# A decoder layer on one core: the mixer's VectorE work moved into PSUM, the division of the softmax moved behind the product with the values

## The chip, the cores and the metric

The kernel runs on one core of a Trainium2 chip. The metric is device time in microseconds (us) of one execution. A core has five engines that work side by side, each through its own instructions strictly in order: TensorE (PE in the profile, with its weight loads as PEld), VectorE (DVE), ScalarE (ACT), GpSimd (POOL) and SyncE (SP), which here issues the DMAs. Matmul results land in PSUM, eight banks of 128 partitions x 512 floats; everything else lies in SBUF.

## The reference, cut to what matters

A layer over 512 tokens of width 1024: a SwiGLU feed-forward network (FFN), a mixer, a second FFN, each with an RMSNorm in front and a residual add. The change is in the mixer alone:

```
p = rmsnorm(x) @ W_in                         # qa, ka, va, qi, ki, wi, cq, ckv, kr
qa, ka, qi, ki = rope(...)                    # x1*c - x2*s, x1*s + x2*c
# group A (Dsa): 8 query heads share one key/value head; an indexer of 16 heads picks 128 keys
score[t,s] = sum_h wi[t,h] * relu(qi[t,h] . ki[s])      # causal; top 128 keys of each query stay
out_A = softmax(qa . ka / 8 on the kept keys) @ va
# group B (Mla): 8 heads, queries and keys from low-rank latents, a shared rotary key
out_B = softmax((qn . kn + rope(qp) . rope(kr)) / sqrt(96), causal) @ v
x = x + concat(out_A, out_B) @ W_out
```

All arithmetic is float32. There are 4 query blocks of 128, so block i has (i+1) key blocks.

## The kernel before, in words

A product of two float32 matrices is done as three fast matmuls (`mm3`, L136, L139, L140) on operands that are cut into a high part (ScalarE rounds, L94) and a low part (the difference, L95 on VectorE or GpSimd). Every weight tile goes through this `split`. The products of probabilities and values and all transposes stay plain float32.

The FFNs lie before 393 us and after 700 us of the span; the mixer is between. Its order is written out by hand in `ORDER`: `q0`..`q7` are the index query projections (two heads of 64 each, for the three blocks that need an index: 384 tokens), `s0`..`s7` their rope and their stacking into operands, `i0`..`i7` the index heads, `T` and `k` the keys, `e` the rotary key, `l0`..`l4` the latents, `K`, `V` keys and values of group B, `A0`..`A3` and `S0`..`S3` the queries of group A, `b` rounds of the top-k search in the background. After the bar `|` come the 16 attention units (units 0 to 7 are Mla heads, 8 to 15 Dsa units, a block i and a half of the heads): `g` builds operands, `s` scores and softmax, `z` the division by the sum, `a` transposes of the probabilities and the product with the values, `o` parts of the output product. The tile framework then decides the order on each engine within what these dependences allow.

What the steps below touch:

- rope (L613 to L629): VectorE multiplies by the cosine out of PSUM into a buffer `f` (L619). The crossed halves times the sine come either from VectorE (L621, L622) or, after a ScalarE copy to SBUF, from GpSimd (L626, L627); the add (L628) is on either.
- stack and doubled (L637, L663): high part on ScalarE, low part on VectorE or GpSimd (L642, L669), quarters moved by DMA or by VectorE copies (L671).
- index heads (L692): two matmuls (L700, L701), relu on ScalarE from PSUM to a buffer `r` (L703, four buffers), multiply by the head's weight and accumulate on VectorE (L704).
- top-k (L709): 16 rounds of MAX8 and MATCH_REPLACE8 (L712, L713) on three score tiles, then L716.
- softmax (L855): VectorE adds mask or index and takes the maximum (L865), ScalarE exponentiates with the sum beside it (L873).
- normalise (L877): reciprocal (L880), then each block's probabilities are multiplied, on VectorE (L885) or GpSimd (L883).
- apply: transposes (L950 of Mla, L986 of Dsa), a copy to SBUF (L899 VectorE, L901 ScalarE), then the product: the values (64 columns) are loaded as weights and the transposed probabilities move, up to 512 columns (L953) or 256 (L991). The result is already turned (value dimension on partitions).

`ON_VECTOR` is a set of names that says which of two engines does an item.

Of the kernel before, what the change touches and what calls it, by code (L numbers as in the profile page):

```python
# [14 lines left out]
P = 128  # L15
# [10 lines left out]
BUFS = dict(pf=5, pr=4, ph=2, ah=7)  # L26
ORDER = """q0 q1 T c s0 r s1 t k q2 v w q3 i0 q4 a s2 i1 s4 q6 i2 q7 s3 q5 s6 s7 e s5 i3 l0 i4 i7 l1 i5 i6 l2 l3 l4 p b3 n0 u A0
A1 b2 K S0 A2 R b2 b2 S1 b2 A3 b3 S3 V S2 |
g0 s0 n1 g1 b2 g2 b2 s1 z0 s2 z1 b2 g3 g4 a0 s3 a1 b2 g5 z2 s4 a2 b2 z4 g6 z3 s5 g7 a3 s6 g8 z5 b2 b2 g9 a4 s7 g10 a5
b2 z6 s8 b2 a6 b2 b2 z7 a7 s9 o0 z8 g11 b2 b2 g12 b20 z9 b2 s10 z10 a8 s11 a9 a10 z11 g13 s12 o1 a11 g14 s13 z12 g15  # L30
s14 z13 s15 a12 z14 b2 o2 a13 a14 z15 a15 o3 o4 o5 b2 b2 o6 b2 o7 b2"""
ON_VECTOR = set("""c0.0 c0.1 c0.2 c0.3 c1.0 c1.2 c10.0 c11.0 c13.0 c14.3 c15.0 c15.1 c15.3 c2.1 c2.3 c3.1 c3.2 c3.3 c4.0 c4.3
c5.1 c6.0 c6.1 c6.2 c6.3 c7.2 gk5 gk7 kf mrA2 mrT mre mrq1 mrq2 mrq3 mrq5 mrq7 oa00 oa01 oa02 oa10 oa20 oa23
oa31 oa32 oa33 ob1 ob2 re rq1 rq2 rq3 rq5 ru1 sA2 sq6 sq7 su1 wA3 wV wl0 wl3 wo0 wo1 wo4 wo5 wo6 wo7 wq1 wq2
wq5 wq6 wq7 z0.0 z0.2 z0.3 z10.0 z10.2 z11.2 z12.0 z12.2 z12.3 z13.0 z13.2 z14.2 z14.3 z15.0 z15.1 z15.2 z2.3
z3.0 z3.1 z3.2 z3.3 z4.2 z4.3 z5.1 z5.2 z6.0 z6.2 z7.0 z7.1 z7.2 z7.3 z8.0 z9.0 z9.1""".split())
# [148 lines left out]
def rows_of(k, col, out):  # L185
    nc = k.nc
    pb = k.tr()
    for t in range(NT):
        nc.tensor.matmul(pb[:, t * P:(t + 1) * P], col[:, t:t + 1].to_broadcast([P, P]), k.ident, start=True, stop=True)
    nc.scalar.activation(out, pb, AF.Copy)  # L190
    return out
# [196 lines left out]
def engine(nc, name):  # L388

    return nc.vector if name in ON_VECTOR else nc.gpsimd  # L390


def add_mixer_weights(k, w_in, w_uq, w_ukv, w_out):
# [9 lines left out]
    lo = lambda name: engine(nc, "w" + name)  # L403
# [11 lines left out]
    def prep_keys():  # L415
        h, l = (w3(x, ND) for x in k.whl())
        for half in range(2):
            src = cell["t"][:, :, 0:128].rearrange("p d (h s c) -> p d h s c", h=2, s=2)[:, :, :, half, :]
            hv, lv = (x[:, :, 64 * half:64 * half + 64].rearrange("p d (h c) -> p d h c", h=2) for x in (h, l))
            k.split(hv, lv, src, lo("T"))  # L420
        return h, l

    def prep_rest():
        h, l = (w3(x, ND) for x in k.whl())
        for a, b, n in ((0, 208, 16), (16, 128, 16), (32, 144, 32), (64, 224, 16), (80, 128, 16), (96, 176, 32)):
            k.split(h[:, :, a:a + n], l[:, :, a:a + n], cell["t"][:, :, b:b + n], lo("t"))
# [4 lines left out]
    def rope_chunk(col, *names):  # L431
# [7 lines left out]
        def prep(j):  # L439
            def f():  # L440
                h, l = (w3(x, ND) for x in k.whl())
                for half in range(2):
                    src = c["r"][:, :, 128 * j:128 * j + 128].rearrange("p d (h s c) -> p d h s c", h=2, s=2)[:, :, :, half, :]
                    hv, lv = (x[:, :, 64 * half:64 * half + 64].rearrange("p d (h c) -> p d h c", h=2) for x in (h, l))
                    k.split(hv, lv, src, lo(names[j]))
# [11 lines left out]
    def plain(col, *names):  # L457
# [8 lines left out]
        def prep(j):  # L466
            def f():
                h, l = (w3(x, ND) for x in k.whl())
                k.split(h, l, c["r"][:, :, j * P:(j + 1) * P], lo(names[j]))
# [749 lines left out]
```

## Time and profile before

| | |
|---|---|
| runs, three | 1062.78 to 1064.68 us, median 1063.2 us |
| the profiled execution | 1066.48 us, of which its span is 1064.7 us |
| PE busy over the span | 1017.1 us (96%) |
| VectorE, ScalarE, GpSimd busy | 511.8, 385.2, 148.2 us |
| mixer | about 393 to 700 us of the span |

The profiled execution is one of its own; its span is what the trace covers, and 1.8 us lie around it. In the FFNs TensorE has no gaps; the stretches with gaps are those of the mixer. A busy share is not a bound: which wait ends last in a stretch is read from the chain of work that ended last.

### The profile page before, as it was taken

Reading aid. Unit: us, or ns where it says so; the run is one execution under the profiler, and the core shown is the slowest. Engines: PE = TensorE matmul, PEld = TensorE weight load, DVE = VectorE, ACT = ScalarE, POOL = GpSimd, SP = SyncE. Lnnn points to the kernel's source line nnn. Section 1 sums busy time; section 2 is a strip of 40 time slices with the busy share of each in tenths; the row PEclk is TensorE's granted clock in tenths of the full one; section 3 lists DMA queues with packets and bytes.
Section 4 is the critical chain, followed back from the end, with each engine's and each line's share of the span. In section 5 each row is a group of like instructions: output and inputs, shape, how many; then the busy total and the mean of one; then the engine's idle time right before and its main releaser. Section 6 shows DMA issues by size and latency. Waiting matters only on the chain.

```text
span 1064.7 us, 12212 instructions
## 1 busy us (share of the span) xinstructions
PE 1017.1 (96%) x4726; PEld 832.1 (78%) x4726; DVE 511.8 (48%) x895; ACT 385.2 (36%) x691; POOL 148.2 (14%) x142
## 2 busy tenths in 40 slices
PE   5999999999999999889889999999999999999997
PEld 3888888888888888768765566888888888888886
DVE  5333332333333336989996768553333233333343
ACT  5322221122222335654367556353222212222222
POOL 1000000000000026533984222000000000000000
PEclk9999999999999999989988999999999999999999
DMA  8232233223323123322251001243323232222302
GB/s 289 77 109 79 79 119 119 79 79 100 108 90 97 40 79 98 119 76 100 85 162 54 6 1 60 83 154 119 119 79 118 81 103 95 79 80 99 118 1 80
DMA packets 83391, 98.84 MB, mean 93 GB/s; under 512 B 9027, under 2 KB 65475, under 8 KB 83333
## 3 DMA queue, kind: packets, MB, share of 16 engines
q1 hardware_dynamic: 83328, 98.06, 28.7%
q8 instruction: 37, 0.61, 0.2%
q14 instruction: 22, 0.17, 0.1%
q10 hardware_dynamic: 4, 0.00, 0.0%
HBM read 91.89 MB, written 2.10 MB: 88 GB/s over the span
## 4 chain that ended last, share of the span: by engine, by line
PE 80%; DVE 12%; ACT 3%; issue 3%; DMA 1%; POOL 1%; SPq 0%; POOLq 0%; DVEq 0%; ACTq 0%
PE ps L136 24%; PE ps L139 24%; PE ps L140 24%; DVE idx L713 2%; DVE s L712 2%; DVE idx L704 1%; PE ps L953 1%; DVE wl L95 1%; DMA raw<-in_w_up_dram 1%; PE ps L991 1%; DVE p L885 1%; PE ps L986 1%; PE ps L950 1%; DVE p L865 1%; PE ps L975 1%
## 5 line engine op out<-in xcount | busy, mean ns | idle before, releaser
L94 ACT ACTIVATE wh<-raw 128x1024 fp32r<-128x1024 f32 (+4 forms) x154 | 140.1, 925 | 386.5 <-PE ps L139 297.4
L95 DVE TENSOR_TENSOR wl<-raw,wh 128x1024 fp32r<-128x1024 f32 (+1 forms) x122 | 145.0, 1192 | 277.3 <-ACT wh L94 276.9
L136 PE MATMUL ps<-xh,wh 128*128 128x512 f32 (+2 forms) x712 | 267.0, 379 | 5.1 <-DVE res L1123 1.7
L139 PE MATMUL ps<-xh,wh 128*128 128x512 f32 (+2 forms) x712 | 268.0, 377 | 1.9 <-DVE xh L95 1.9
L140 PE MATMUL ps<-xh,wl 128*128 128x512 f32 (+2 forms) x712 | 267.9, 377 | 1.3 <-POOL wl L95 0.9
L136 PEld LDWEIGHTS ps<-xh,wh 128*128 128x128 f32 x712 | 134.4, 190 | 30.0 <-DVE f L622 2.1
L140 PEld LDWEIGHTS ps<-xh,wl 128*128 128x128 f32 x712 | 135.1, 190 | 25.2 <-POOL wl L95 1.3
L139 PEld LDWEIGHTS ps<-xh,wh 128*128 128x128 f32 x712 | 135.2, 190 | 25.0 <-DVE xh L95 2.2
L136 PE MATMUL ps<-wh,h 128*128 128x512 f32 x272 | 105.9, 389 | 0.0
L140 PE MATMUL ps<-wh,h 128*128 128x512 f32 x272 | 105.8, 389 | 0.0
L139 PE MATMUL ps<-wl,h 128*128 128x512 f32 x272 | 105.8, 389 | 0.0
L95 POOL TENSOR_TENSOR wl<-raw,wh 128x512 fp32r<-128x512 f32 (+5 forms) x32 | 43.3, 1374 | 403.7 <-ACT wh L94 399.1
L327 DVE TENSOR_TENSOR t<-ps,t 128x512 f32<-128x512 f32 x44 | 30.4, 692 | 141.3 <-PE ps L140 141.3
L94 ACT ACTIVATE w<-raw 128x1024 fp32r<-128x1024 f32 x32 | 34.0, 1061 | 118.3 <-PE ps L139 118.3
L136 PE MATMUL ps<-xh,w 128*128 128x512 f32 x176 | 68.5, 389 | 0.0
L140 PE MATMUL ps<-xh,w 128*128 128x512 f32 x176 | 68.5, 389 | 0.0
L139 PE MATMUL ps<-xh,w 128*128 128x512 f32 x176 | 68.5, 389 | 0.0
L283 POOL TENSOR_TENSOR fr<-tot,mhalf 128x1 f32<-128x1 f32 x12 | 7.3, 614 | 415.6 <-DVE tot L1166 360.1
L140 PEld LDWEIGHTS ps<-wh,h 128*128 128x128 f32 x272 | 51.0, 188 | 10.7
L136 PEld LDWEIGHTS ps<-wh,h 128*128 128x128 f32 x272 | 51.1, 188 | 10.6
L139 PEld LDWEIGHTS ps<-wl,h 128*128 128x128 f32 x272 | 51.1, 188 | 10.5
L95 DVE TENSOR_TENSOR w<-raw,w 128x1024 fp32r<-128x1024 f32 x32 | 39.2, 1225 | 29.6 <-ACT w L94 29.6
(214 smaller groups left out, 1349.5 us busy)
## 6 DMA issues: line engine op xcount, KB each, us to landing
raw<-in_w_up_dram SPq DMA_DIRECT2D x22, 1024.0 KB, 5.2
raw<-in_w_gate_dram SPq DMA_DIRECT2D x21, 1024.0 KB, 5.2
raw<-in_w_down_dram SPq DMA_DIRECT2D x20, 1024.0 KB, 5.0
raw<-in_w_in_dram SPq DMA_DIRECT2D x8, 1024.0 KB, 5.2
raw<-in_w_out_dram SPq DMA_DIRECT2D x4, 1024.0 KB, 5.3
res<-in_x_dram SPq DMA_DIRECT2D x4, 512.0 KB, 7.0
raw<-in_w_down_dram SPq DMA_DIRECT2D x4, 512.0 KB, 3.6
raw<-in_w_ukv_dram SPq DMA_DIRECT2D x2, 1024.0 KB, 4.9
```

The costliest lines, as they stand in the source:

```text
L94: self.nc.scalar.activation(hi, src, AF.Copy)
L95: (lo_engine or self.nc.vector).tensor_tensor(out=lo, in0=src, in1=hi.bitcast(F32), op=ALU.subtract)
L136: i = mm(out, wh, xh, start=first, stop=False)
L139: mm(out, wh, xl, start=False, stop=False)
L140: return i, mm(out, wl, xh, start=False, stop=last)
L327: nc.vector.tensor_tensor(out=u, in0=pu, in1=g, op=ALU.mult)
L704: nc.vector.scalar_tensor_tensor(out=score[i], in0=r, scalar=wt[:, i, h:h + 1], in1=cm(i) if h == 0 else score[i], op0=ALU.mult, op1=ALU.add)
L712: nc.vector.max(out=m8, in_=score[i])
L713: nc.vector.match_replace(out=score[i], in_to_replace=m8, in_values=score[i], imm_value=TAKEN)
L865: nc.vector.tensor_tensor_reduce(out=e, in0=p[:, :n], in1=bias, scale=1.0, scalar=-3.0e38, op0=ALU.add, op1=ALU.max, accum_out=mx[:, c:c + 1])
L885: nc.vector.tensor_scalar(out=e, in0=e, scalar1=rc[:, c:c + 1], scalar2=None, op0=ALU.mult)
L950: nc.tensor.transpose(p[:, i * P:(i + 1) * P], probs[i][:, j * P:(j + 1) * P], k.ident)
```

## The change

1. Rope is done in place in PSUM, with four VectorE instructions: two halves times sine into `f`, the PSUM tile times cosine, the add. No rope has a ScalarE copy or a GpSimd part any more, except the rotary key `e`, which is wholly on GpSimd from an SBUF copy.
2. The index heads' relu is written back to PSUM and VectorE accumulates from there; the `r` buffers go.
3. The low parts of all mixer weights (L95 of `wl`) are on GpSimd; 15 of them were on VectorE.
4. The low parts of stacked and doubled operands, of `pe` and of group B's queries are on VectorE out of PSUM; group B's key low parts are all on GpSimd. Group B's queries stay in PSUM with no copy. The quarters of the keys' low parts are moved by ScalarE and by DMA.
5. The `z` step goes. The product runs on probabilities that are not divided; `divided` takes the reciprocal and multiplies the product's result on VectorE, 12 times (4 pairs of Mla heads, 512 wide, and 8 Dsa units, 256 wide).
6. In the product the transposed probabilities are the weights (128 x 128) and the values move (64 columns). The result has queries on partitions and is transposed afterwards: 16 transposes for Mla (new L944) and 16 for Dsa (new L985).
7. The attention's SBUF buffers `h` go from 7 to 8.

```diff
-    def rope(p, tab, name, n0=0):
+    def rope(p, tab, n0=0, eng=nc.vector):
...
-        nc.vector.tensor_tensor(out=a, in0=p, in1=c, op=ALU.mult)
-        if "m" + name in ON_VECTOR:
-            nc.vector.tensor_tensor(out=b[lower], in0=p[upper], in1=s[upper], op=ALU.mult)
-            nc.vector.tensor_tensor(out=b[upper], in0=p[lower], in1=s[lower], op=ALU.mult)
-        else:
-            x = f32()[:, n0:]
-            nc.scalar.activation(x, p, AF.Copy)
-            nc.gpsimd.tensor_tensor(out=b[lower], in0=x[upper], in1=s[upper], op=ALU.mult)
-            nc.gpsimd.tensor_tensor(out=b[upper], in0=x[lower], in1=s[lower], op=ALU.mult)
-        engine(nc, name).tensor_tensor(out=a, in0=a, in1=b, op=ALU.add)
-        return a
+        eng.tensor_tensor(out=b[lower], in0=p[upper], in1=s[upper], op=ALU.mult)
+        eng.tensor_tensor(out=b[upper], in0=p[lower], in1=s[lower], op=ALU.mult)
+        eng.tensor_tensor(out=p, in0=p, in1=c, op=ALU.mult)
+        eng.tensor_tensor(out=p, in0=p, in1=b, op=ALU.add)
+        return p
...
-                r = fr()[:, :n]
-                nc.scalar.activation(r, p, AF.Relu)
-                nc.vector.scalar_tensor_tensor(out=score[i], in0=r, scalar=wt[:, i, h:h + 1],
+                nc.scalar.activation(p, p, AF.Relu)
+                nc.vector.scalar_tensor_tensor(out=score[i], in0=p, scalar=wt[:, i, h:h + 1],
...
-            k.split(kh[r], kl[r], kf[pr][r], engine(nc, f"gk{h}"))
-            k.split(qh[r], ql[r], Mla.qf[r], engine(nc, f"gq{h}"))
+            k.split(kh[r], kl[r], kf[pr][r], nc.gpsimd)
+            k.split(qh[r], ql[r], Mla.qf[r])
...
-            po = Mla.po[64:128] if odd else Mla.po[0:64]
+            po = Mla.po.rearrange("p (i e c) -> p i e c", i=NT, e=2)
...
-                nc.tensor.matmul(po[:, j * P:], vb[j][:, h, :], t[:, j * P:], start=(j == 0), stop=(j == NT - 1))
+                for i in range(j, NT):
+                    nc.tensor.matmul(po[:, i, odd, :], t[:, i * P:(i + 1) * P], vb[j][:, h, :],
+                                     start=(odd == i == j == 0), stop=(odd == 1 and i == j == NT - 1))
             if odd:
+                o = divided(Mla.po, self.sm.rearrange("p a b -> p (a b)"))
+                p = k.tr()
+                for i in range(NT):
+                    nc.tensor.transpose(p[:, i * P:(i + 1) * P], o[:, i * P:(i + 1) * P], k.ident)
...
-                t = t.rearrange("p (a b q) -> p a b q", a=2, b=2)
-                for b in range(2):
-                    nc.tensor.matmul(po[64 * b:64 * b + 64, 0:256].rearrange("p (a q) -> p a q", a=2), va[:, j, :],
-                                     t[:, :, b, :], start=(j == 0), stop=(j == i))
+                for h in range(4):
+                    nc.tensor.matmul(po[:, 64 * h:64 * h + 64], t[:, h * P:(h + 1) * P], va[:, j, :], start=(h == j == 0), stop=(h == 3 and j == i))
+            o = divided(po, self.sm)
+            p = k.tr()
+            for e in range(2):
+                nc.tensor.transpose(p[:, e * P:(e + 1) * P], o[:, e * P:(e + 1) * P], k.ident)
+
+    def divided(po, sm):
+        rc = sums_of_two()
+        n = po.shape[1] // 64
+        rc = rc.rearrange("p a b -> p (a b)")[:, :n]
         nc.vector.reciprocal(out=rc, in_=sm)
...
+        o = turned()[:, :64 * n]
+        nc.vector.tensor_tensor(out=o.rearrange("p (a c) -> p a c", c=64), in0=po.rearrange("p (a c) -> p a c", c=64),
+                                in1=rc.unsqueeze(2).to_broadcast([P, n, 64]), op=ALU.mult)
+        return o
```

VectorE's order in the middle of the index heads before (`idx` are the score tiles, `r` the relu buffers, `ps` PSUM tiles, `wl` a weight's low part):

```order
L704 SCALAR_TENSOR_TENSOR idx_2657<-r_2909,wt,idx_2657 128x256
L704 SCALAR_TENSOR_TENSOR idx_2658<-r_2915,wt,idx_2658 128x384
L95 TENSOR_TENSOR wl_3032<-raw_2489,wh_3031 128x8x64 x2
L704 SCALAR_TENSOR_TENSOR idx_2659<-r_2921,wt,idx_2659 128x512
L704 SCALAR_TENSOR_TENSOR idx_2657<-r_2980,wt,idx_2657 128x256
L619 TENSOR_TENSOR f_3129<-ps_2863,tab_2644 128x384
L704 SCALAR_TENSOR_TENSOR idx_2658<-r_2986,wt,idx_2658 128x384
L704 SCALAR_TENSOR_TENSOR idx_2659<-r_2992,wt,idx_2659 128x512
```

And the same place after, where two ropes run among the accumulations:

```order
L612 TENSOR_TENSOR f_2994<-ps_2924,tab_2644 64x384
L613 TENSOR_TENSOR f_2994<-ps_2924,tab_2644 64x384
L612 TENSOR_TENSOR f_3101<-ps_2863,tab_2644 64x384
L613 TENSOR_TENSOR f_3101<-ps_2863,tab_2644 64x384
L614 TENSOR_TENSOR ps_2924<-ps_2924,tab_2643 128x384
L686 SCALAR_TENSOR_TENSOR idx_2656<-ps_2964,wt,idx_2656 128x256
L686 SCALAR_TENSOR_TENSOR idx_2657<-ps_2969,wt,idx_2657 128x384
L614 TENSOR_TENSOR ps_2863<-ps_2863,tab_2643 128x384
L686 SCALAR_TENSOR_TENSOR idx_2658<-ps_2974,wt,idx_2658 128x512
L615 TENSOR_TENSOR ps_2924<-ps_2924,f_2994 128x384
```

The weights' low parts have left VectorE, the ropes' other halves and adds have come, and the accumulations read PSUM tiles.

TensorE's order in two Dsa units before (`p` are probabilities, `h` the copied transposes, `va` the values, `kah` and `kal` the keys of the next scores):

```order
L986 MATMUL ps_4947<-ident,p_4820 128x128 x4
L991 MATMUL ps_4946<-h_4952,va 64x256 x2
L986 MATMUL ps_4961<-ident,p_4891 128x128 x4
L991 MATMUL ps_4960<-h_4966,va 64x256 x2
L986 MATMUL ps_4970<-ident,p_4891 128x128 x4
L975 MATMUL ps_4989<-kah,qa_3861 128x384
L976 MATMUL ps_4989<-kal,qa_3861 128x384
```

And after, a Dsa unit of two key blocks, from its first transpose to the next unit's scores:

```order
L977 MATMUL ps_4989<-ident,p_4868 128x128 x4
L981 MATMUL ps_4988<-va,h_4994 128x64 x4
L977 MATMUL ps_5000<-ident,p_4868 128x128 x4
L981 MATMUL ps_4988<-va,h_5005 128x64 x4
L985 MATMUL ps_5015<-ident,h_5013 128x128 x2
L965 MATMUL ps_5022<-kah,qa_4032 128x384
L966 MATMUL ps_5022<-kal,qa_4032 128x384
```

The product takes four instructions in the order (each is two passes on the engine) where it took two, and the unit ends with transposes (L985) of what VectorE divides; nothing stands between the last product and them.

## Rows read from the trace of the kernel before

**Rows 1.** Windows: us, busy (x) of PE, PEld, DVE, ACT, POOL; PEclk, DMA, GB/s.

```profile
426.00:480.00 54.00, 45.94 (x218) 39.01 (x217) 49.59 (x66) 31.75 (x66) 23.95 (x15) 0.94 0.35 101
480.00:557.00 77.00, 68.85 (x321) 56.71 (x320) 76.94 (x190) 36.78 (x61) 57.61 (x46) 0.96 0.37 115
557.00:602.00 45.00, 41.64 (x193) 26.82 (x192) 35.53 (x115) 31.34 (x84) 19.83 (x22) 0.91 0.13 37
602.00:680.00 78.00, 73.25 (x394) 51.65 (x395) 48.30 (x140) 38.94 (x113) 13.61 (x17) 1.00 0.15 48
```

**Rows 2.** Chain that ended last, by line, in those four windows.

```profile
by line: DVE idx L704 23.6%; issue 22.5%; DVE wl L95 6.6%; PE ps L700 5.0%; PE ps L701 4.4%; ACT r L703 4.2%; PE ps L139 4.1%; PE ps L136 4.1%; PE ps L140 3.8%; DVE f L619 3.7%; DMA qst<-h 3.4%; DVE f L622 3.1%; DVE h L642 2.5%; DVE f L628 
by line: DVE idx L713 29.4%; DVE s L712 24.9%; DVE wl L95 9.3%; issue 8.2%; DVE idx L716 4.4%; DVE f L619 4.1%; DVE kf L792 3.0%; DVE idx L704 2.9%; DVE p L865 2.1%; DVE lat L735 1.8%; ACT wh L94 1.5%; DVE f L628 1.3%; DVE scol L611 1.3%; P
by line: DVE p L885 21.6%; PE ps L953 12.6%; PE ps L950 11.4%; ACT p L873 10.9%; DVE p L865 10.4%; PE ps L935 6.6%; PE ps L936 5.2%; PE ps L937 5.1%; DVE h L899 3.8%; DMA st<-pe 3.8%; issue 3.6%; SPq L632 2.5%; DVE s L880 1.0%; ACT h L901 0
by line: PE ps L136 14.0%; PE ps L139 13.7%; PE ps L140 13.5%; PE ps L991 12.7%; PE ps L986 11.0%; PE ps L953 10.0%; PE ps L975 7.2%; PE ps L976 6.0%; ACT h L901 3.5%; PE ps L950 3.0%; DVE h L899 2.5%; ACT p L94 1.3%; DVE res L1123 0.9%; is
```

**Rows 3.** VectorE where the attention begins.

```profile
554.43 1.48 DVE L716 TENSOR_SCALAR idx<-idx 128x512 f32<-128x512 f32 x1
555.83 0.28 DVE L865 CUSTOM_DVE_ANT_0 p<-ps,cmask 128x128 f32<-128x128 f32 x1
```

**Rows 4.** VectorE before the first accumulation: start, us, what.

```profile
420.57 0.68 DVE L95 TENSOR_TENSOR wl<-raw,wh 128x512 fp32r<-128x512 f32 x1
...
422.33 1.58 DVE L671 CAST kil<-kil 32x512 fp32r<-32x512 f32 x2
...
424.20 0.85 DVE L671 CAST kal<-kal 32x512 fp32r<-32x512 f32 x2
425.08 1.30 DVE L95 TENSOR_TENSOR wl<-raw,wh 128x512 fp32r<-128x512 f32 x2
426.29 1.67 DVE L704 SCALAR_TENSOR_TENSOR idx<-r,wt,cmask 128x256 f32<-128x256 f32 x3
```

**Rows 5.** VectorE by form, 426.25 to 556.9: instruction xcount | busy us, mean ns | idle before.

```profile
L704 DVE SCALAR_TENSOR_TENSOR idx<-r,wt,idx 128x512 f32<-128x512 f32 x15 | 14.8, 988 | 0.0
L704 DVE SCALAR_TENSOR_TENSOR idx<-r,wt,idx 128x384 f32<-128x384 f32 x15 | 12.0, 800 | 0.1
...
L704 DVE SCALAR_TENSOR_TENSOR idx<-r,wt,idx 128x256 f32<-128x256 f32 x15 | 10.0, 670 | 0.0
...
L95 DVE TENSOR_TENSOR wl<-raw,wh 128x1024 fp32r<-128x1024 f32 x5 | 8.3, 1669 | 0.8 <-ACT wh L94 0.8
...
L95 DVE TENSOR_TENSOR wl<-raw,wh 128x512 fp32r<-128x512 f32 x5 | 4.4, 904 | 0.0
L619 DVE TENSOR_TENSOR f<-ps,tab 128x512 f32<-128x512 f32 x6 | 4.0, 672 | 0.0
...
L619 DVE TENSOR_TENSOR f<-ps,tab 128x384 f32<-128x384 f32 x5 | 2.8, 551 | 0.0
L621 DVE TENSOR_TENSOR f<-f,tab 64x512 f32<-64x512 f32 x1 | 2.7, 2710 | 0.1
...
L735 DVE SCALAR_TENSOR_TENSOR lat<-ps,g_q_lat,lat 128x512 fp32r<-128x512 f32 x3 | 2.2, 742 | 3.3 <-ACT lat L734 3.3
...
L619 DVE TENSOR_TENSOR f<-f,tab 128x512 f32<-128x512 f32 x1 | 0.7, 693 | 0.0
```

**Rows 6.** TensorE: a product of Mla, weight loads of transposes, products of Dsa.

```profile
578.99 1.07 PE L953 MATMUL ps<-h,xh 128*64 128x512 f32 x2 [0.32 <-ACT h L901]
...
598.65 1.07 PEld L950 LDWEIGHTS ps<-ident,p 128*128 128x128 f32 x10 [0.17 <-issue]
...
624.53 0.65 PE L991 MATMUL ps<-h,va 128*64 128x256 f32 x4 [0.69 <-ACT h L901]
```

**Rows 7.** TensorE's waits, 600 to 680: us in total, times, longest.

```profile
PE ps L991 <- ACT h L901: 2.4, 3, 1.0
PE ps L991 <- DVE h L899: 1.7, 2, 0.9
```

More of the change, by code (lines that the diff above doesn't have):

```diff
@@ L182, in rstd_of, with rows_of @@
     return col, m
-def rows_of(k, col, out):
+def rows_of(k, col, out=None):
     nc = k.nc
@@ L189, in rows_of @@
         nc.tensor.matmul(pb[:, t * P:(t + 1) * P], col[:, t:t + 1].to_broadcast([P, P]), k.ident, start=True, stop=True)
+    if out is None:
+        return pb
     nc.scalar.activation(out, pb, AF.Copy)
@@ L401, in w3 @@
         return x.rearrange("p (a b) -> p a b", a=a)
-    lo = lambda name: engine(nc, "w" + name)
+    lo = nc.gpsimd
     cell = {}
@@ L635, in quarters, with stack @@
         return [x[32 * q:32 * q + 32] for q in range(4)]
-    def stack(x, make, name, n0=0):
+    def stack(x, make, n0=0):
         out = [make()[:, n0:] for _ in range(2)]
         l = f32r()[:, n0:]
-        nc.scalar.activation(out[0], x, AF.Copy)
-        engine(nc, name).tensor_tensor(out=l, in0=x, in1=out[0].bitcast(F32), op=ALU.subtract)
+        k.split(out[0], l, x)
         nc.scalar.activation(out[1], x, AF.Copy)
@@ L661, in mixer, with doubled @@
     cm = lambda i: k.cmask[:, 384 - P * i:]
[L663 removed]
+    def doubled(x, hi, lo, q, copy):
         o = 1 - q
[L666 removed]
+        k.split(hi, lo, x)
         for e in (0, 2):
             nc.scalar.activation(quarters(hi)[o + e], quarters(x)[q + e], AF.Copy)
[L669 removed]
         for e in (0, 2):
[L671 removed]
+            copy(quarters(lo)[o + e], quarters(lo)[q + e])
     def values(x):
@@ L685, in rotary_key @@
     def rotary_key(x):
-        scaled(tk, v.rows1)
-        x = rope(x, tk, "re")
+        x = rope(x, v.tk, 0, nc.gpsimd)
         h, l = f32r(), f32r()
@@ L755, in norm_rows @@
     def norm_rows(j):
-        v.rows1 = rows_of(k, v.col1, row_tile())
+        rows = rows_of(k, v.col1)
+        v.ta = scaled(ta, rows, True)
+        v.tk = scaled(tk, rows)
     def index_keys(j):
-        v.ta = scaled(ta, v.rows1, True)
-        v.x1 = rope(v.t1, v.ta, "rT")
-        doubled(v.x1, kih, kil, 1, nc.vector)
-    def attention_keys(j):
-        doubled(v.x1, kah, kal, 0, nc.gpsimd)
+        x = rope(v.t1, v.ta)
+        doubled(x, kih, kil, 1, lambda o, i: nc.scalar.activation(o, i, AF.Copy))
+        doubled(x, kah, kal, 0, mv)
     def rest_out(j):
@@ L774, in index_stack @@
     def index_stack(j):
-        stacks[j] = stack(rope(pq.pop(j), ta, f"rq{j}", P), qst, f"sq{j}", P)
+        stacks[j] = stack(rope(pq.pop(j), ta, P), qst, P)
     def keys_b(j):
@@ L790, in keys_b_out @@
             x = mp.tile([P, T], F32, tag="kf", name=k.name("kf"), bufs=8)
-            if "kf" in ON_VECTOR:
-                nc.vector.tensor_tensor(out=x, in0=p, in1=rows, op=ALU.mult)
-            else:
-                nc.scalar.activation(x, p, AF.Copy)
-                nc.gpsimd.tensor_tensor(out=x, in0=x, in1=rows, op=ALU.mult)
+            nc.vector.tensor_tensor(out=x, in0=p, in1=rows, op=ALU.mult)
             kf.append(x)
@@ L812, in rotary_b_out @@
         for g, p in enumerate(v.pab):
-            x = rope(p, tb, f"ru{g}")
+            x = rope(p, tb)
             h, l = (mp.tile([P, T], F32R, tag="kf", name=k.name("pe"), bufs=8) for _ in range(2))
-            k.split(h, l, x, engine(nc, f"su{g}"))
+            k.split(h, l, x)
             pe.append((h, l))
@@ L829, in stack_a @@
     def stack_a(j):
-        qa[2 * j], qa[2 * j + 1] = stack(rope(pa.pop(j), v.ta, f"rA{j}"), mkqa, f"sA{j}")
+        qa[2 * j], qa[2 * j + 1] = stack(rope(pa.pop(j), v.ta), mkqa)
     def values_b(j):
@@ L853, in mixer, with softmax @@
     turned = k.junk = lambda: ap.tile([P, T], F32, tag="h", name=k.name("h"), bufs=BUFS["ah"])
-    def softmax(scores, scale, neg=None):
-        mx, sm, nb = (small(4) for _ in range(3))
+    def softmax(scores, sm, scale, neg=None):
+        mx, nb = (small(4) for _ in range(2))
         out = []
@@ L938, in score @@
                 out.append((p, cm(i)))
-            self.probs = softmax(out, *v.scale_b)
+            if h % 2 == 0:
+                Mla.sm = sums_of_two()
+            self.sm = Mla.sm
+            self.probs = softmax(out, self.sm[:, :, h % 2], *v.scale_b)
         def apply(self):
@@ L1010, in out_part @@
             out_done(t, half, p, part == 0)
-    do = dict(g=lambda j: units[j].gather(), s=lambda j: units[j].score(), z=lambda j: normalise(j),
+    do = dict(g=lambda j: units[j].gather(), s=lambda j: units[j].score(),
               a=lambda j: units[j].apply(), o=out_part, n=lambda j: k.weights(ids[f"n{j}"]), b=background)
```

76 lines of the change are left out of this document (29 added, 47 removed).

## The prediction

> **What bounds the kernel now.** First I read which engine works in each stretch of the mixer, in windows [rows 1]. From 480 to 557 us VectorE is busy 76.94 of 77.00 us; from 426 to 480 it is busy 49.59 of 54, TensorE 45.94. From 602 on the picture turns: TensorE 73.25 of 78 us, VectorE 48.30. Between (557 to 602) TensorE has 41.64 of 45 us, VectorE 35.53. [...]
>
> Busy shares don't say who sets the end, so I then read the chain of waits of each window [rows 2]. From 426 to 480 its longest part is VectorE's accumulations L704 (23.6%) and the low parts L95 (6.6%); from 480 to 557 it is the top-k (L713 29.4%, L712 24.9%) and L95 (9.3%). From 557 to 602 the largest part is the normalise pass L885, 21.6% of 45.0 us = 9.7 us. From 602 on TensorE's own lines follow one another and no line of the division is named in what the row shows. So there are three stages: VectorE bounds to 557, VectorE and ScalarE between TensorE's work bound to 602, TensorE bounds from there. The change relieves the first two and loads the third.
>
> That the first stage hands on what it gains is seen where the attention begins [rows 3]: the last top-k instruction L716 starts at 554.43, and the first maximum L865 follows it at 555.83 on the same in-order engine. Whatever VectorE finishes earlier, the attention starts earlier.
>
> **The change part by part.** *Before the first accumulation.* In the 5.7 us ahead of 426.29 VectorE does 0.68 + 1.30 us of weights' low parts and 1.58 + 0.85 us of quarter copies [rows 4], 4.4 us that all leave it (GpSimd, ScalarE and DMA take them). ScalarE's quarter copies now stand before the first index matmul. I take -4 us; bounds 0 (something else is as late, GpSimd's weights first) and -5.
>
> *The VectorE stage, 426.25 to 556.9.* What leaves: 10 low parts of weights, 8.3 + 4.4 = 12.7 us [rows 5]. What comes: 61 instructions of rope, stack, `pe` and group B's query low parts where 30 stood; 31 more at 0.55 us (the 384-wide multiply out of PSUM, 551 ns; the 512-wide takes 672) are +17, and the one 64x512 multiply of 2710 ns, whose sources lie in SBUF, is then an ordinary 0.7: -2. Net +15. What gets cheaper: the 45 accumulations take 988, 800 and 670 ns with both sources in SBUF; an instruction of the same kind with one source in PSUM, L735 at 128x512, took 742 ns in the same stretch, in which GpSimd was busy most of the time (57.61 of 77 us, [rows 1]). So I price the 512-wide accumulation out of PSUM at 0.74, and the narrower ones by the step of the multiplies (672 - 551 = 121 ns) at 0.62 and 0.50: 15 x (0.25 + 0.18 + 0.17) = -9. Sum: -12.7 + 15 - 9 = -7. The rows overlap a little at their ends, so I count -6 of time. If the accumulations don't get cheaper it is about +2; if L716 (1.48 us for the widest, [rows 3]) loses its surplus over the multiply's 0.67 as well, in two or three instructions, it is -9.
>
> GpSimd gets 15 more weights' low parts and loses its share of the ropes, of the stacks and of the normalise blocks (30 of 64). It is busy 57.61 of 77 us at its worst, so I cost that at nothing; what hides it is that weights are prepared two items ahead. If that cover is gone, TensorE waits for low parts, and the 12.7 us that VectorE spent on ten of them bound it; with 19 us of GpSimd idle in that window I leave this end out of the range.
>
> *Attention of Mla, 557 to 602.* The normalise pass leaves the chain: -9.7 us at most. The product of probabilities and values: a pair of passes over 512 columns takes 1.07 us [rows 6], 2.1 ns a column, so 8 heads x 1280 columns are 21.4 us. After it there are 80 products of two passes that are limited by the weight load; ten loads of 128x128 take 1.07 us [rows 6], so 160 x 0.107 = 17 us, and with the entry into each group of them some 20: -1. The 16 new transposes are 16 x 0.107 = +1.7. Each pair of heads now ends with a reciprocal and a 512-wide multiply that TensorE waits for, since its next instructions are those transposes; waits for one copy were 0.7 to 1.0 us [rows 6, 7], so two instructions and two hand-offs are about 1.2, four times: +4.8. The sum is -4. Bounds: -9.7 (waits hidden) and +6 (L885 lay beside TensorE work that ends just behind it).
>
> *Attention of Dsa and output product, from 602.* The products of 256 columns took 0.65 us for a group of four [rows 6], and there are 20 groups: 13.0 us. After it, 160 passes x 0.107 = 17.1, and an entry of 0.04 for each group: +4.9. New transposes: 16 x 0.107 = +1.7. Then waits. Before, 5 of the 20 groups waited for their copy, 2.4 + 1.7 = 4.1 us in all [rows 7], 0.8 each (one of 0.69 stands in [rows 6]). After, the order puts each product straight behind its transposes and each unit's final transposes straight behind its last product, with the reciprocal and the multiply between, eight times. I take half of the eight to be exposed at 0.8: +3.2. The sum is +10. Bounds: +5 (the waits hidden and the loads a little better) and +20 (all eight and ten more copies exposed).
>
> *Sum.* -4 - 6 - 4 + 10 = -4 us. The profiled execution was 1066.48 us (span 1064.7 and 1.8 around it), which makes it 1062.5; the median of the runs lies 3.3 lower, and there the forecast is **1059 us**.
>
> [...]
>
> **The rivals.** (1) *The tail decides.* In the Dsa units every copy and every division is exposed, because TensorE is the bound there and nothing is queued between. Its place is from 602 on, its price +20 in place of +11, and it decides as soon as more than the -14 of the first stages is given back: -14 + 20 = +6, 1069 us. For it: the order, and chain rows that are TensorE's alone. Against it: only a quarter of the copies are exposed before, with the same pairs of instructions.
>
> (2) *The gain is not handed on.* PSUM tiles are held longer (through four rope steps and two copies of the stack, through the relu, and the queries through two heads), there are eight banks, and TensorE starves or VectorE waits for products late. Then the first two terms give -3 in place of -10: +3, 1066 us. For it: TensorE already loses time from 426 to 480, and the chain has 22.5% issue there. Against it: TensorE has 8 us free in each of these two windows.
>
> (3) *Everything is hidden.* The division runs beside other units, the Dsa stage costs +5, Mla gives -8, the first two terms -11: -14, and less of the attention runs at the lower clock: 1046 to 1049 us. For it: the largest part of the chain from 557 to 602 leaves VectorE. Against it: VectorE's in-order queue puts the division behind maxima of later units.
>
> [...]
>
> **How the numbers follow.** Forecast case 0.42 (1059, own range 1053 to 1065), rival 1 0.22, rival 2 0.14, rival 3 0.17, rival 4 0.05. Runs of this kernel differ by 0.2%, 2 us, so faster means under 1061.1 and slower over 1065.3. Of the forecast case 0.29 lie below, 0.09 within and 0.04 above; rival 3 is all faster; of rivals 1, 2 and 4 together 0.05 faster, 0.07 the same, 0.29 slower. That makes faster 0.51, the same 0.16, slower 0.33. The range runs from rival 3's middle, 1047, to a little over rival 1's, 1071.
>
> **What would show each step.** Accumulations out of PSUM at 0.48 to 0.75 us beside a busy GpSimd, and the first L865 near 546 us of the span, show the first stage right. Means of 0.8 to 1.0 us, or VectorE idle in 426 to 546, would show it wrong. The product's weight loads at 0.107 each, in groups of four to sixteen, show the loads; gaps before the new transposes, 12 in all, and before the products show the waits. The forecast is wrong if the first L865 does not move, if those gaps add up to over 15 us, or if the attention stretch grows by less than 3 us.

## The result and the profile after

The changed kernel takes 1094.5 us (median, 1093.6 to 1098.4) against 1063.7 for the kernel before on the same chip: ratio 1.0297, interval 1.027 to 1.0323. It is 31 us slower, and the forecast was 1059. Its profiled span is 1091.8 us, 27.1 longer than before.

First the place. These are VectorE's rows where the accumulations begin and where the attention begins (start, us, what), answering [rows 4] and [rows 3]:

```profile
417.34 1.01 DVE L686 SCALAR_TENSOR_TENSOR idx<-ps,wt,cmask 128x256 f32<-128x256 f32 x2 [0.76 <-ACT ps L685]
...
544.08 0.29 DVE L843 CUSTOM_DVE_ANT_0 p<-ps,cmask 128x128 f32<-128x128 f32 x1
```

The first accumulation comes at 417.3 in place of 426.3, the first maximum at 544.1 in place of 555.8, 11.7 us earlier. Not all of that is the change's. The same residual add near the end of the first FFN, which the change doesn't touch, stands here in the two traces (before, then after):

```profile
385.17 0.69 DVE L363 SCALAR_TENSOR_TENSOR res<-ps,res 128x512 f32<-128x512 f32 x1 [2.03 <-PE ps L140]
```

```profile
381.87 0.69 DVE L362 SCALAR_TENSOR_TENSOR res<-ps,res 128x512 f32<-128x512 f32 x1 [2.03 <-PE ps L137]
```

The profiled execution of the kernel before was 3.3 us late already there; two kernels that are the same up to that point (e6 and e7 below) have this add at 382.5 and 382.6. So the change gains 11.7 - 3.3 = 8.4 us by the time that the attention starts (forecast 10), and all the loss lies behind.

The next rows are windows of the stretch from the first maximum to the last transposes of the normed input of the second FFN, of the kernel before and of the changed one (us from:to, us, busy of PE, PEld, DVE, ACT, POOL, granted clock, DMA share, GB/s):

```profile
555.83:702.54 146.71, 136.10 (x710) 96.99 (x711) 101.85 (x293) 80.86 (x222) 36.84 (x43) 0.97 0.19 59
```

```profile
544.08:726.41 182.33, 155.47 (x890) 136.39 (x891) 84.28 (x260) 79.53 (x216) 22.04 (x15) 0.88 0.13 40
```

The stretch is 35.6 us longer. VectorE and GpSimd do less in it, as meant. TensorE is busy 19.4 us more and idle 16.2 us more (182.33 - 155.47 = 26.9 against 10.6). The windows of the changed kernel that lie wholly at one level show a granted clock of 1.00 (589.33 to 623.46) or of 0.50 (two are below); a mean of 0.88 between these two means that 2 x 0.12 x 182 = 44 us of it ran at the lower level; before it was 2 x 0.03 x 147 = 9 us. (After the stretch the two kernels do the same FFN; in the changed one 3.2 us of its first products fall behind the end of the stretch, so from the first maximum on the loss is 35.6 + 3.2 = 38.8 us; 38.8 - 8.4 = 30.4 agrees with the 31 of the runs.)

TensorE's waits in it (us in total, times, longest), answering [rows 7]:

```profile
PE ps L981 <- ACT h L881: 6.7, 7, 3.0
PE ps L985 <- DVE h L864: 4.1, 8, 0.5
PE ps L981 <- DVE h L879: 3.5, 4, 0.9
PE ps L938 <- ACT h L881: 3.4, 2, 2.6
PE ps L938 <- DVE h L879: 3.3, 3, 1.4
PE ps L944 <- DVE h L864: 3.1, 4, 0.8
```

L985 and L944 wait for the division (7.2 us, all twelve times), L981 and L938 for a copy of transposes (16.9 us). How that looks is seen in TensorE's timeline, in the first and the third of three Dsa units:

```profile
614.83 0.60 PE L977 MATMUL ps<-ident,p 128*128 128x128 f32 x4
616.12 1.10 PE L981 MATMUL ps<-va,h 128*128 128x64 f32 x8 [0.69 <-ACT h L881]
617.74 0.44 PE L985 MATMUL ps<-ident,h 128*128 128x128 f32 x2 [0.52 <-DVE h L864]
...
622.15 0.60 PE L977 MATMUL ps<-ident,p 128*128 128x128 f32 x4
623.53 1.97 PE L981 MATMUL ps<-va,h 128*128 128x64 f32 x8 [0.78 <-DVE h L879]
625.29 1.06 PE L977 MATMUL ps<-ident,p 128*128 128x128 f32 x4
627.04 1.97 PE L981 MATMUL ps<-va,h 128*128 128x64 f32 x8 [0.69 <-ACT h L881]
629.52 0.69 PE L985 MATMUL ps<-ident,h 128*128 128x128 f32 x2 [0.52 <-DVE h L864]
```

Transposes, a wait, the product, a wait, transposes of the result: in these units the engine stands still before each product and before the last transposes. In the kernel before, other products often stood in that place:

```profile
619.69 0.60 PE L986 MATMUL ps<-ident,p 128*128 128x128 f32 x4
620.04 0.48 PE L136 MATMUL ps<-wh,ob 128*128 128x512 f32 x1
...
621.06 0.63 PE L140 MATMUL ps<-wh,ob 128*128 128x512 f32 x2
621.61 0.65 PE L991 MATMUL ps<-h,va 128*64 128x256 f32 x4
```

That product, the first of the Dsa units, starts 65.8 us after the first maximum, and 72.0 us after it in the changed kernel (616.12 above). The matmuls ahead of it are the same but for the new form of the product and its transposes. So the Mla stage lost 6.3 us and everything behind it 32.6.

In the rows of the changed kernel, from 623 on the same eight passes take 1.97 us in place of 1.10, and four transposes 1.06 in place of 0.60: the clock has fallen to the lower level. Two windows of the changed kernel lie wholly there, each behind a long wait for a copy of transposes:

```profile
574.78 3.76 PE L938 MATMUL ps<-xh,h 128*128 128x64 f32 x20 [2.56 <-ACT h L881]
```

```profile
654.42 1.97 PE L981 MATMUL ps<-va,h 128*128 128x64 f32 x8 [3.00 <-ACT h L881]
```

```profile
575.67:589.33 13.66, 12.09 (x52) 11.11 (x52) 4.46 (x14) 4.02 (x11) 0.00 (x0) 0.50 0.01 2
...
654.18:667.83 13.65, 12.89 (x47) 11.31 (x48) 3.87 (x13) 4.75 (x13) 0.00 (x0) 0.50 0.00 1
```

So the clock fell behind waits of both kinds: behind the five of 0.5 to 0.8 us ahead of 623.5 in the Dsa units, and behind single waits for copies of 2.6 and 3.0 us.

The product itself grew too. Its rows in the stretch (instruction xcount | busy us, mean ns | waits), before and after:

```profile
L953 PE MATMUL ps<-h,xh 128*64 128x256 f32 (+3 forms) x64 | 21.6, 457 | 2.0 <-DVE h L899 1.7 <-ACT h L901 0.3
...
L991 PE MATMUL ps<-h,va 128*64 128x256 f32 x80 | 11.4, 396 | 4.1 <-ACT h L901 2.4 <-DVE h L899 1.7
```

```profile
L981 PE MATMUL ps<-va,h 128*128 128x64 f32 x160 | 25.1, 316 | 10.3 <-ACT h L881 6.7 <-DVE h L879 3.5
L938 PE MATMUL ps<-xh,h 128*128 128x64 f32 x160 | 22.2, 293 | 6.7 <-ACT h L881 3.4 <-DVE h L879 3.3
```

It keeps TensorE busy for 47.3 us in place of 33.0, part of it at the lower clock, and waits for copies for 16.9 us in place of 6.1.

### The profile page after: what moved, and what is told of

It is laid out like the page before. It is cut to its first block, busy times and chain, and to the rows that moved or that the text cites. A ratio compares the mean times of both kernels' runs of the same rounds, so it can differ in the third digit from the quotient of the medians.

```text
span 1091.8 us, 12487 instructions
## 1 busy us (share of the span) xinstructions
PE 1035.6 (95%) x4934; PEld 871.3 (80%) x4934; DVE 483.0 (44%) x882; ACT 377.4 (35%) x680; POOL 109.8 (10%) x95
## 4 chain that ended last, share of the span: by engine, by line
PE 83%; DVE 10%; ACT 4%; issue 2%; DMA 1%; POOL 0%; SPq 0%; POOLq 0%; ACTq 0%; DVEq 0%
PE ps L133 25%; PE ps L136 25%; PE ps L137 25%; PE ps L981 2%; DVE idx L695 2%; DVE s L694 2%; PE ps L938 2%; ACT p L851 1%; DVE p L843 1%; PE ps L977 1%; DVE h L864 1%; ACT h L881 1%; PE ps L934 1%; DMA raw<-in_w_gate_dram 1%; DVE f L612 0%
## 5 line engine op out<-in xcount | busy, mean ns | idle before, releaser
L92 DVE TENSOR_TENSOR wl<-raw,wh 128x1024 fp32r<-128x1024 f32 (+1 forms) x102 | 122.7, 1204 | 276.9 <-ACT wh L91 276.6
L92 POOL TENSOR_TENSOR wl<-raw,wh 128x512 fp32r<-128x512 f32 (+5 forms) x52 | 75.3, 1470 | 512.3 <-ACT wh L91 508.4
L326 DVE TENSOR_TENSOR t<-ps,t 128x512 f32<-128x512 f32 x44 | 30.4, 691 | 145.4 <-PE ps L137 145.4
L137 PEld LDWEIGHTS ps<-wh,h 128*128 128x128 f32 x272 | 51.0, 188 | 10.6
L136 PEld LDWEIGHTS ps<-wl,h 128*128 128x128 f32 x272 | 51.1, 188 | 10.6
```

What stands on the lines that cost most here:

```text
L92: (lo_engine or self.nc.vector).tensor_tensor(out=lo, in0=src, in1=hi.bitcast(F32), op=ALU.subtract)
L136: mm(out, wh, xl, start=False, stop=False)
L137: return i, mm(out, wl, xh, start=False, stop=last)
L326: nc.vector.tensor_tensor(out=u, in0=pu, in1=g, op=ALU.mult)
```

## The experiments

Times are medians; each is compared with the kernel before on the same chip (1063.7 to 1064.7 us). Two experiments that lie less than about 4 us apart are not told apart unless the text says so, since the runs of one kernel spread over 1 to 7 us.

**e1: the two halves of the change apart.** The attention of before in the changed kernel:

```diff
-g0 s0 n1 g1 b2 g2 b2 s1 s2 ...
+g0 s0 n1 g1 b2 g2 b2 s1 z0 s2 z1 ...
-                for i in range(j, NT):
-                    nc.tensor.matmul(po[:, i, odd, :], t[:, i * P:(i + 1) * P], vb[j][:, h, :], ...
+                nc.tensor.matmul(po[:, j * P:], vb[j][:, h, :], t[:, j * P:], start=(j == 0), stop=(j == NT - 1))
```

> The changed kernel with the attention of the kernel before: the normalise pass is back (64 blocks, on the engines of before), the product has the values as weights again, no division and no transposes behind it. Ropes and relu in PSUM and all low parts of mixer weights on GpSimd stay. Theory A (the loss of 31 us lies wholly in the attention, and the projections gain what the first maximum shows, 555.8 to 544.1 us = 11.7): 1063.7 - 11.7 = 1052, within 3. Theory B (part of the loss comes from the projection part, through PSUM tiles held or GpSimd late with weights in the attention): 1060 or more.

Measured: 1057.2 us, ratio 0.9932 (0.9918 to 0.9947), between the two cases. **e2** is the other half, the new attention in the kernel before.

> The kernel before with only the attention of the changed one: division behind the product, values that move, transposes of the result, no normalise pass. Theory A: the stretch from the first maximum to the second FFN grows as in the changed kernel (146.6 to 182.3 us, +36), so 1063.7 + 36 = 1099, within 5. Theory B (the two parts hurt each other): 1063.7 + 31 - x, under 1090.

Measured: 1098.5 us, ratio 1.0324 (1.0307 to 1.0342), the first case. The loss is the attention's alone (+34 us in the kernel before, 37 on top of e1); the projections gain 7. Case A of e1 had counted on 11.7, which is too much by what the kernel before was late in its trace: without that the maximum moves by 8.4 in e1, too. From the first maximum to the end e1 then takes 511.4 us against 508.9, at a clock of 0.94 against 0.97 in the stretch; that the lower clock is the reason is not shown (v3 below did not win it back).

**e3: no wait for the division.** The result's transposes read a tile that is ready; the attention's output is left out.

```diff
-                    nc.tensor.transpose(p[:, i * P:(i + 1) * P], o[:, i * P:(i + 1) * P], k.ident)
+                    nc.tensor.transpose(p[:, i * P:(i + 1) * P], k.ident, k.ident)
```

> The changed kernel, in which the 32 transposes of the result read the identity in place of the divided result, so TensorE doesn't wait for reciprocal and multiply (both are still done; the attention's output is left out). If the waits for the division are the cause: their 7.2 us (4.1 at the Dsa units, 3.1 at the Mla pairs) and what they cost in clock go, 1094.5 - 7 to -20 = 1075 to 1088. If the cause is the product itself (its 320 passes and its waits for copies): 1094.5 - 3 to -7, 1088 to 1092, and the granted clock of the stretch stays near 0.88.

Measured: 1071.2 us, less than either case allowed. Taking away 7.2 us of waits takes away 23.4. Its window of the stretch:

```profile
545.26:702.93 157.67, 140.89 (x890) 126.83 (x891) 82.83 (x259) 78.47 (x215) 22.09 (x15) 0.94 0.14 43
```

The same 890 matmuls are now 14.6 us less busy, at a clock of 0.94 in place of 0.88, and idle time is 10.1 us less. So the wait is paid for at least twice: as idle time, and as slower work afterwards. (Without it, the output products need not wait for the division either.)

**e4: 128 moving columns for each load in place of 64**, half of each result unused:

```diff
-                    nc.tensor.matmul(po[:, 64 * h:64 * h + 64], t[:, h * P:(h + 1) * P], va[:, j, :], ...
+                    nc.tensor.matmul(po[:, P * h:P * h + P], t[:, h * P:(h + 1) * P], va[:, j, :], ...   # va: the values twice
```

> The changed kernel with 128 moving columns in each product in place of 64 (Mla: the values of both heads of a pair; Dsa: the values twice), half of each result unused; the weights loaded and the number of passes stay, one more PSUM bank for each pair and 4 more multiplies of half the width. If TensorE falls to its lower clock because the product's passes move few columns for each load: the granted clock of the stretch rises from 0.88 to 0.95 or more, and the time falls by 5 to 15 us although twice the columns move (1080 to 1090). If the clock falls because of the waits: the clock stays at 0.88 and the time stays or rises, 1093 to 1103.

Measured: 1086.6 us, 8 less although twice the columns move:

```profile
545.60:719.99 174.39, 145.49 (x890) 125.82 (x891) 84.16 (x266) 79.73 (x218) 22.03 (x15) 0.96 0.14 43
```

This is the first case by both of its numbers. TensorE's waits for the division are still there (6.2 us), but the clock is 0.96; so the waits alone do not decide the clock. The time fell by far less than the 30 us fewer at the lower level (14 in place of 44). Twice the columns cost time as well, and part of the slower work may have lain beside waits for other engines; how much is which is not shown.

**e5: the division's result is used later.** The transposes and the split of a unit are issued at the next unit's product:

```diff
+            finish()
             o = divided(po, self.sm)
-            p = k.tr()
-            for e in range(2): ...
+            unfinished.append(last)      # last(): the transposes and the split
```

> The changed kernel with the transposes of a unit's divided result and their split issued at the next unit's product (before an output part at the latest), in place of right behind the own product, so that the division runs beside scores and transposes. If the wait of TensorE for the division is what costs 23 us (with the clock that it drags down): 1071 to 1076, as without the wait. If leaving the result out helped for another reason (less data, PSUM): 1085 to 1095.

Measured: 1084.6 us (1080.2 to 1086.4). The first case, which I held, missed: waits for the division fell to 2.5 us, but the waits for copies rose to 18.1 and the clock stayed at 0.88. So the 10 us that it won are hardly the clock's. Why it won less than e3 is open: in e3 the output products don't wait for the division either, and here the waits for copies are longer.

**e10: useless work in the wait.** Between the last product and the transposes of each unit stand four (Mla) or three (Dsa) matmuls into a PSUM tile that nobody reads:

```diff
+                last = fill(4, last)      # matmul(p, kah[:, :P], kah), queued behind the product
                 p = k.tr()
```

> The changed kernel with useless TensorE work put where it waits for the division: four matmuls of 512 columns at each Mla pair and three at each Dsa unit, 40 in all, about 0.23 us each, into a PSUM bank that nobody reads. If a good part of the loss is the lower clock that follows these waits: the lower clock in the stretch falls from 45 to under 25 us and the time falls by 4 to 12 us in spite of the added work, 1082 to 1090. If the loss is the latency alone: the same or more, 1094 to 1100.

Measured: 1084.4 us, as in the first case: 10 less than the changed kernel with 40 matmuls more. The transposes are queued behind the fill. In TensorE's timeline the fill takes the place of the wait, and the transposes start 1.70 us after the product in place of 1.62:

```profile
610.93 1.10 PE L991 MATMUL ps<-va,h 128*128 128x64 f32 x8 [0.69 <-ACT h L881]
611.84 0.95 PE L886 MATMUL ps<-kah 128*128 128x512 f32 x3
612.63 0.39 PE L996 MATMUL ps<-ident,h 128*128 128x128 f32 x2
```

The window of its stretch has a clock of 0.94:

```profile
542.63:713.48 170.85, 152.75 (x930) 133.05 (x931) 83.49 (x260) 79.34 (x217) 22.07 (x15) 0.94 0.14 44
```

That makes 21 us at the lower level in place of 44. A wait for a copy of 2.5 us still stands where the first long stretch began, but the clock is back up after 3.4 us (at 579.6), not after 13.7:

```profile
573.62 2.44 PE L946 MATMUL ps<-xh,h 128*128 128x64 f32 x20 [2.54 <-ACT h L881]
```

The transposes follow no sooner and the waits for copies fell by 1.4 us only (16.9 to 15.5), so about 10 us of the loss are the lower clock, after what the fill itself costs. Either edit alone, this one (0.94) or e4's (0.96), brings the clock of the stretch up from 0.88.

**e9: the division ahead again, the product still turned.**

```diff
-        nc.vector.tensor_tensor(out=o.rearrange(...), in0=po.rearrange(...), in1=rc.unsqueeze(2).to_broadcast([P, n, 64]), op=ALU.mult)
+        nc.vector.tensor_copy(o, po)      # and the normalise pass ahead of the product, as before
```

> The changed kernel with the normalise pass back ahead of the product (on the engines of before) and a plain VectorE copy of the result in place of reciprocal and multiply; the values still move and the result is still transposed. If the turned product with its transposes is what costs, and the place of the division little: 1090 to 1098, as the wait for a copy stands where the wait for the division stood. If the division behind the product is what costs: 1070 to 1080.

Measured: 1098.2 us, at the edge of the first case. The division's new place is no loss: with the old one the kernel is not faster (3.6 us slower, with intervals of the ratios that overlap: 1.0296 to 1.0337 against 1.027 to 1.0323). What costs is the product that leaves its result to be turned, with a step of VectorE between product and transposes, be it a copy or a division.

**e8 and e12: what is left without that wait.** e8 is e3 and e4 together; e12 is e3 without the 32 transposes (the split reads the product where it lies, so turning and dividing the output are left out).

```diff
-            p = k.tr()
-            for e in range(2):
-                nc.tensor.transpose(p[:, e * P:(e + 1) * P], k.ident, k.ident)
+            p = po
```

> The changed kernel with both edits: 128 moving columns in each product, and result transposes that read the identity (the division is done but not waited for, the attention's output left out). If the wider product only saves lower clock, and without the wait little lower clock is left (17.8 us of the stretch): 1066 to 1072, at most 5 under the kernel without the wait. If the two work apart: 1071 - 8 = 1063. What is left over the projection part alone (1057) is then the price of the product's extra passes, of the 32 transposes and of its waits for copies.

> The changed kernel without the 32 transposes of the result: the split reads the product where it lies, undivided and not turned (the division is done but not waited for; turning and dividing the attention's output are left out). Against the kernel whose transposes read the identity (1071.2): if the transposes and their place between products cost little, 1068 to 1071; if they carry much of what is left of the turned product, 1062 to 1067. The rest over 1057.2 is the price of the product's passes and waits for copies.

Measured: e8 1068.1 us (1065.7 to 1073.1), e12 1069.3, both in their first cases. The transposes' own work is worth 2 us, the wider product 3 once the wait is gone, neither clear of the spread. The other 12 us over e1 are the product's passes and its waits for copies: in e12's trace the product is busy for 41.4 us (32.8 in e1) and waits for copies for 13.5 (5.5 in e1), 16.6 more together, against which stand 2.5 us of waits for the normalise pass that e1 has and e12 has not. No run put other products between transposes and product again, so what of this the order could hide is not tested.

**e6, e7, e11: the parts of the projections.** e6 is the kernel before with the relu left in PSUM, e7 with all low parts of mixer weights on GpSimd; e11 is e1 with those low parts on the engines of before.

```diff
-                nc.scalar.activation(r, p, AF.Relu)
-                nc.vector.scalar_tensor_tensor(out=score[i], in0=r, ...
+                nc.scalar.activation(p, p, AF.Relu)
+                nc.vector.scalar_tensor_tensor(out=score[i], in0=p, ...
```

```diff
-    lo = lambda name: engine(nc, "w" + name)
+    lo = lambda name: nc.gpsimd
```

> The kernel before with one edit: the relu of the index heads stays in PSUM and VectorE accumulates from there. Theory A (the accumulations are slowed by GpSimd because both sources lie in SBUF): they take 0.74, 0.61 and 0.48 us in the mean in place of 0.99, 0.80 and 0.67, the first maximum comes 5 to 9 us earlier, and the time falls by 3 to 7 us (1057 to 1061). Theory B (they are as long from PSUM, or PSUM tiles held longer starve TensorE): 1063 or more.

> The kernel before with one edit: all low parts of the mixer's weights on GpSimd. Theory A: VectorE loses 12.7 us of low parts before the attention, but GpSimd is busier beside the accumulations, whose means go up; net -3 to -8 on the first maximum, time 1058 to 1063. Theory B (GpSimd, which has the ropes too, comes late with weights): 1066 or more.

> The changed kernel with the attention of before (1057.2) and the low parts of mixer weights on the engines of before, 15 on VectorE; ropes, stacks and relu in PSUM stay as changed. If moving the low parts pays once GpSimd is free of ropes: 12.7 us more on VectorE before the attention, of which part shows, 1060 to 1066. If VectorE has room, or they cost as much through GpSimd: 1055 to 1059.

Measured: e6 1058.5 us, ratio 0.9937 (0.9923 to 0.9952); e7 1069.2, ratio 1.004; e11 1066.6, 9.4 over e1. By their times e6 is its first case and e7 its second; e11 lies 0.6 above its first. The accumulations of e6, then of e7, by form on VectorE (instruction xcount | busy us, mean ns | idle):

```profile
L702 DVE SCALAR_TENSOR_TENSOR idx<-ps,wt,idx 128x512 f32<-128x512 f32 x15 | 11.2, 744 | 0.0
L702 DVE SCALAR_TENSOR_TENSOR idx<-ps,wt,idx 128x384 f32<-128x384 f32 x15 | 9.1, 610 | 0.0
...
L702 DVE SCALAR_TENSOR_TENSOR idx<-ps,wt,idx 128x256 f32<-128x256 f32 x15 | 7.2, 477 | 0.0
```

```profile
L704 DVE SCALAR_TENSOR_TENSOR idx<-r,wt,idx 128x512 f32<-128x512 f32 x15 | 15.3, 1017 | 0.0
L704 DVE SCALAR_TENSOR_TENSOR idx<-r,wt,idx 128x384 f32<-128x384 f32 x15 | 14.8, 986 | 0.0
L704 DVE SCALAR_TENSOR_TENSOR idx<-r,wt,idx 128x256 f32<-128x256 f32 x15 | 10.7, 715 | 0.1
```

Out of PSUM they take what was forecast (0.74, 0.62, 0.50) to 0.02 us, beside the same GpSimd work. With more work on GpSimd the ones out of SBUF get slower still (986 against 800 in [rows 5]). These and other instructions with their sources in SBUF (the tables' L586 1542 ns against 686, the widest L716 3.79 us against 1.48) eat all that VectorE is relieved of: from the first accumulation to the first maximum it is busy for 124.7 us in e7 and for 125.1 in the kernel before. The parts need one another: low parts on GpSimd lose 5 us alone and gain 9 (e1 against e11) once ropes have left GpSimd and the accumulations read PSUM. What one source in PSUM is worth is seen in e6, whose edit leaves GpSimd's instructions as they are: at 128x512 the accumulation took 744 ns with one source in SBUF, and 988 [rows 5] with both there.

**v1 and v3: two tries at more**, both on e1. v1 queues each top-k round of the second half behind a maximum of the softmax; v3 puts 40 useless matmuls before the attention's first transposes.

```diff
+                if i == 1 and k.maxed is not None:
+                    k.after(m, k.maxed)
```

```diff
+            last = fill(40, k.scored) if h == 0 else None
```

> The changed kernel with the attention of before (as e1_projection_part, 1057.2), and each top-k round of the second half queued on VectorE behind a maximum of the softmax that stands ahead of it in the program, so that VectorE starts the attention some 8 rounds (3.3 us each, the page of before) earlier and does them in its idle time there. If the attention starts late because VectorE does top-k first: the first maximum comes 15 to 25 us earlier and the time falls by 5 to 15 us, 1042 to 1052. If the start is set by the operands of group B (latents, keys) or the rounds fill what was idle anyway: 1055 to 1060.

> The changed kernel with the attention of before (1057.2), and 40 useless matmuls of 512 columns (9 us) between the first scores and the first transposes of the attention, where TensorE waits for VectorE's top-k. If the lower clock of 533 to 550 us in that kernel costs time in the attention's beginning: 1052 to 1056. If TensorE doesn't bound there, or the fill is itself late: 1057 to 1064.

Measured: v1 1062.5 us, v3 1063.7, both slower than e1; v1 lies above both of its cases, v3 in the second. In v1 the first maximum comes at 532, 12 us earlier, but the stretch takes 161.5 us in place of 145.7; TensorE has waits of 5.5 us for a normalise block and 6.1 us for a DMA of operands there. v3's fill left the clock of its stretch at 0.95 (0.94 in e1). Filling one long wait did not help where filling twelve short ones did.

The fastest version measured is e1, 1057.2 us, not told apart from e6, 1058.5; both beat the kernel before, by 0.6 to 0.7%, and the changed one.

## Why the prediction was wrong, by its steps

*Before the first accumulation*: -4 forecast (0 to -5). From the residual add to the first accumulation it is 41.1 us before and 35.5 after, -5.6. Right in sign and nearly in size, but not by the parts that I counted: the low parts, 2.0 of my 4.4 us, are worth 0.8 to 1.4 (36.3 with them back on VectorE in e11, 39.8 with them alone in e7). The quarter copies were the other 2.4. That the rest is ropes and stacks, which I had not counted, is argued only.

*The VectorE stage*: -6 forecast, -2.8 measured (126.7 against 129.5 us from first accumulation to first maximum). The accumulations' -9 came as worked out, and alone give 6 us of time (e6). VectorE's work in the stage fell by 9.8 us (7 were forecast), from 125.1 to 115.3, but its idle time there rose from 4.5 to 11.4. From 426 to 480 TensorE is full in its place:

```profile
426.00:480.00 54.00, 52.44 (x265) 45.36 (x263) 45.02 (x97) 30.17 (x65) 23.67 (x16) 1.00 0.35 105
```

It is busy 52.44 of 54 us there (45.94 in [rows 1]), VectorE 45.02. Relieved on VectorE, the stage paid until TensorE was full. Together the two terms are -8.4 against -10.

*Mla -4, Dsa and output product +10*: this is the step that failed. Together they were +6; measured are +38.8: +6.3 in the Mla stage and +32.6 behind it, outside both of their bounds (+6 and +20). The time that TensorE stands before the new transposes was sized well, 3.1 us at the pairs and 4.1 at the Dsa units against 4.8 and 3.2. But the wait was priced as that idle time alone, and two terms beside it were mis-sized:

- The wait for the division. 8.0 us were forecast for it, and its removal is worth 23.4 (e3): 7.2 are the idle time of the rows, and about 10 the lower clock, which I let matter only as a gain (rival 3): 44 us of the 182 ran at the lower level. About 6 are left. That output products come later in a tail with little else ready would fit them (e3 frees them, e5 doesn't); no run shows this alone, and it stays open.
- The waits for copies, which I put at nothing more. In the Dsa units 5 of 20 products waited before, for 4.1 us [rows 7], and 11 of 20 after, for 10.2; at Mla it was 2.0 before and 6.7 after. I had carried over "a quarter is exposed" with "the same pairs of instructions". But before, other products stood between many of the transposes and their product; after, the order showed them back to back, and I discounted it.
- The product's passes: -1 and +4.9 were forecast with the new groups' entries, +4 in all; measured are +14.3 (33.0 to 47.3), of which 8.6 stay where the wait is gone (e12 against e1). A group of eight took 1.10 us at the higher clock where 8 x 0.107 + 0.04 = 0.90 was counted; the 0.04 for a group's entry was my estimate, and no run shows it.
- The normalise pass was credited with -9.7 us of the Mla stage because it was 21.6% of the chain there. With it back ahead of the turned product (e9) the time is not told apart from the changed kernel's, 3.6 us more. The chain ran through the pass; that TensorE's work lay close beside it is argued only.

From e1 to the changed kernel the experiments go in steps, whose sum is the whole difference because each is measured from the one before: +12 for the product's passes and copies (1057.2 to e12's 1069.3), +2 for the transposes (to e3's 1071.2), +23 for the wait behind it (to 1094.5).

My own sign of being wrong came true: the gaps before the new transposes and before the products add up to 24.1 us, where I had set 15 as the limit.

*The rivals.* Rival 1, the tail decides, was right in sign and in its place, and too small there (+20 where +32.6 came); it was given 0.22. (It says "in place of +11" where the sum has +10; nothing hangs on that.) Rival 2 did not occur as priced: -8.4 us reached the attention's start and not -3, though VectorE does stand idle longer in its stage. Rival 3, everything is hidden, is the opposite of what came. The 0.05 of rival 4 stood for accumulations that take as long out of PSUM as out of SBUF, with +2 in place of -6 for the VectorE stage. That did not occur: they took 744, 610 and 477 ns in e6 against 988, 800 and 670 [rows 5], and the multiply, which now reads and writes PSUM, 688 against 672:

```profile
L614 DVE TENSOR_TENSOR ps<-ps,tab 128x512 f32<-128x512 f32 x7 | 4.8, 688 | 0.0
```

## What to carry to other kernels

A step's share of the chain of waits was only an upper bound of what its removal gave (the normalise pass: 9.7 us of the chain, and 3.6 us, not told apart, between e9 and the changed kernel); look which engine lies close beside it. Where TensorE bounds a stretch, a change that puts a step of another engine between two of its instructions, in a unit with nothing queued between, is priced by the wait times its count and then again by what the clock does afterwards: here 7.2 us and about 10. Rows of the same form at either clock level (1.10 and 1.97 us here) give that second price. Before a gain is read off two traces, a row ahead of the change should stand at the same time in both; here 3.3 of 11.7 us were the executions' own. And when two engines share one pool of work, test each move both alone and with the others: here one of them lost 5 us alone and gained 9 in company.

## What had not been expected

Not expected by the prediction, though by the notes written ahead of each run: adding 40 useless matmuls made a kernel 10 us faster, and moving twice the columns for each weight load made it 8 us faster, with the granted clock of the stretch up from 0.88 to 0.94 and 0.96. The clock does not rank the kernels, though: e5 is as fast as e10 at 0.88. The lowest of all, 0.86, belongs to e9.
